# Backbone kernel on one core: where and when both mixers' first loads land, and the order of the first token tiles

## The chip, the cores and the metric

The program runs on one of the eight cores of a Trainium2 chip. A core has five engines with queues of their own: TensorE (PE, matmuls and transposes by an identity), VectorE (DVE), ScalarE (ACT), GpSimd (POOL) and SyncE (SP, which here issues loads only). DMA queues move data between HBM and the on-chip memory. An engine works its queue in order and waits at semaphores. The metric is the time of one execution on the device in microseconds, the median of several runs.

## The reference

Two layers over 512 latent tokens and 256 context tokens of width 1024, in float32. Each layer is a mixer, then a mixture of experts.

```python
for l in range(DEPTH):
    mod  = (silu(c) @ w_ada[l] + b_ada[l])          # six vectors of 1024; modc likewise from c_ctx
    h  = rms_norm(x, norm_w[l, 0]) * (1 + mod[1]) + mod[0]
    hc = rms_norm(ctx, norm_w[l, 0]) * (1 + modc[1]) + modc[0]
    yc, s_f, s_b = token_mixer(hc, w_in[l], ...)     # layer 1: only the states are wanted
    y, _, _      = token_mixer(h, w_in[l], ..., s_f, s_b)
    x = x + mod[2] * (y @ w_out[l])
    x = x + mod[5] * hier_moe(modulate(rms_norm(x, norm_w[l, 1]), mod[3], mod[4]))
    # layer 0 does the same two steps for ctx
return rms_norm(x, final_norm_w)

def token_mixer(h, w_in_l, ...):
    p = h @ w_in_l                                   # 1024 x 4096
    bg, cg, hv, q, zf_f, zf_b, iv, g = jnp.split(p, PROJ_SPLITS, axis=-1)
    # a gated short convolution of bg, cg, hv; a two-way recurrence of q, zf_f, zf_b, iv, gated by g
```

## The kernel before, in words

The 768 tokens are six tiles of 128 (four of x, two of ctx). A projection in float32 precision is made of three products of rounded parts: `split_w` (L312 to L323) loads a weight chunk of 512 KB into a `raw` tile, ACT casts it to a rounded high part (L319), and DVE or POOL subtracts that to get the low part (L322); both lie in a `hilo` tile. There are two `raw` buffers and four `hilo` buffers. The input is split likewise: `modulated` (L264) writes the high part of a token tile into H[0] = HA and H[1] = HB (four of the eight 128-wide blocks each) by ACT, and a low part by a POOL subtraction (L283), from a `mod` tile that DVE (and in layer 1 ACT for the first four blocks) makes. `proj_N` (L337) then does 24 matmuls for one token tile.

Each mixer starts with the same stage: normalise the tokens, transpose them on PE, modulate them, and project them on the value columns of w_in (`val`, L590, into Vn). I call it the value stage. After it come the head, gate and convolution projections, then the output projection, the router and the experts.

*Start of layer 0.* `setup` (L39) zeroes `rows` and fills it by seven small loads on SP's queue. `norm_first` (L285) loads each token tile on ACT's queue into one of two `xin` buffers, squares it on ACT (L256), makes its reciprocal root on DVE and POOL (L248, L249), multiplies on DVE (L261), transposes (L298) and copies to XT (L299), all six tiles ahead of the rest. `ada_step` (L199), eight times, loads a 1 MB slice of w_ada on SP's queue into one of three `adaw` buffers and multiplies it by the conditioning; after the eighth the result is transposed into the modulation columns (L222 to L242). Only behind these loads stand the first four chunks of w_in (`nat(6)`, L587).

*Start of layer 1.* The experts of layer 0 leave two rows for each token in `yb`, written by POOL's scatters. `combine` (L1577) loads them and adds both to X (L1588); `square`, `norm_next` (L302) and `modulated` follow. The order on DVE is written by hand (`manual_schedule`), so that tile i + 2 is added, and tile i + 1 multiplied and transposed, around the modulation of tile i. For the other engines the framework's scheduler sets the order, mostly that of the program. Two of the four weight chunks are split on DVE, two on POOL among the first tiles.

## Time and profile before

| | us |
|---|---|
| median of 3 runs (2002.50 to 2003.29) | 2002.74 |
| profiled execution, its own time | 1996.57 |
| its span in the trace | 1994.8 |
| mean granted TensorE clock | 0.945 |
| PE busy | 1700.2 (85% of the span) |
| DVE, ACT, POOL busy | 914.0, 458.2, 394.3 |

The span is that of one profiled execution; busy times are of its engines. A row of a timeline gives start, length, engine, source line and operation with output<-inputs; in brackets stands how long the engine was idle before it and what ended that. Several equal instructions are merged to one row (x12). The ends of matmuls are modelled, so a row of matmuls looks longer than the distance to the next row's start. The granted clock is a share of the full 2.4 GHz.

### The profile page before, as it was taken

How to read it: one execution, taken by the hardware profiler on the slowest of the kernel's cores; microseconds unless marked ns; L12 is line 12 of the kernel's file. 1: busy time of each engine (PE TensorE's matmuls, PEld its weight loads, DVE VectorE, ACT ScalarE, POOL GpSimd, SP SyncE). 2: the span in 40 equal slices, each digit the busy share in tenths (PEclk: the TensorE clock that was granted, in tenths of full speed). 3: DMA queues.
4: the chain of work that ended last, by engine and by line, in shares of the span. 5: the costliest groups of instructions: out<-in, count | busy, mean ns of one | idle time of the engine just before them, and what ended most of it. 6: DMA issues, size and time to landing. Idle time of an engine off the chain costs nothing. (4 is left out here: it accounts for less than half of the span.)

```text
span 1994.8 us, 33498 instructions
## 1 busy us (share of the span) xinstructions
PE 1700.2 (85%) x13488; PEld 1098.2 (55%) x13488; DVE 914.0 (46%) x2141; ACT 458.2 (23%) x897; POOL 394.3 (20%) x308
## 2 busy tenths in 40 slices
PE   5998999999968999888875899898968898888885
PEld 2766778798843444333332688777754344334342
DVE  4425255635664132222322637666563644445444
ACT  3512223323212122122211533333320100110011
POOL 1502212111122111111110632222111211111110
PEclk8999999999988999999987899999987999999998
DMA  7376562263489979999997322114478989999995
GB/s 276 101 271 212 179 212 76 76 242 90 168 326 374 418 317 379 417 416 418 417 419 298 135 82 57 54 43 157 137 280 324 417 342 417 418 417 418 417 418 241
DMA packets 141513, 542.35 MB, mean 272 GB/s; under 512 B 17394, under 2 KB 66720, under 8 KB 85417
## 3 DMA queue, kind: packets, MB, share of 16 engines
q1 hardware_dynamic: 118408, 466.17, 59.1%
q10 hardware_dynamic: 15040, 55.08, 8.0%
q0 software_dynamic: 7904, 18.90, 2.5%
q8 instruction: 108, 1.77, 0.4%
q14 instruction: 53, 0.43, 0.1%
HBM read 530.95 MB, written 15.96 MB: 274 GB/s over the span
## 5 line engine op out<-in xcount | busy, mean ns | idle before, releaser
L1230 PE MATMUL acc<-w,xT 128*32 128x256 f32 (+1 forms) x3360 | 378.4, 454 | 59.1 <-DVE xT L1213 34.6
L1230 PEld LDWEIGHTS acc<-w,xT 128*32 128x32 f32 (+1 forms) x3360 | 135.2, 119 | 260.6 <-issue 159.0
L322 POOL TENSOR_TENSOR hilo<-raw,hilo 128x1024 fp32r<-128x1024 f32 x64 | 157.3, 2463 | 436.4 <-ACT hilo L319 396.7
L333 PE MATMUL acc<-HA,hilo 128*128 128x384 f32 (+1 forms) x960 | 204.7, 355 | 0.0
L333 PE MATMUL acc<-HB,hilo 128*128 128x384 f32 (+1 forms) x960 | 202.4, 353 | 0.0
L333 PEld LDWEIGHTS acc<-HA,hilo 128*128 128x128 f32 x960 | 168.8, 189 | 16.2 <-issue 4.2
L333 PEld LDWEIGHTS acc<-HB,hilo 128*128 128x128 f32 x960 | 171.0, 190 | 9.2 <-issue 0.8
L1250 ACT COPY au<-acc 128x256 f32<-128x256 f32 (+1 forms) x69 | 31.1, 453 | 594.3 <-PE acc L1230 551.9
L345 PE MATMUL acc<-hilo,HA 128*128 128x512 f32 x504 | 131.2, 412 | 12.8 <-POOL HA L283 6.3
L1189 POOL DMA_INDIRECT xb<-h,idx x63 | 65.7, 1043 | 385.7 <-PE pS L1211 357.1
L345 PE MATMUL acc<-hilo,HB 128*128 128x512 f32 x504 | 125.8, 398 | 3.9 <-DVE hilo L322 3.6
L345 PEld LDWEIGHTS acc<-hilo,HA 128*128 128x128 f32 x504 | 97.9, 198 | 41.0 <-POOL HA L283 7.5
L1274 DVE SCALAR_TENSOR_TENSOR au<-w,gt,au 32x256 f32<-32x256 f32 (+2 forms) x102 | 58.6, 577 | 114.1 <-ACT au L1273 111.7
L319 ACT CAST hilo<-raw 128x1024 fp32r<-128x1024 f32 x80 | 83.5, 1049 | 119.1 <-PE acc L345 27.5
L345 PEld LDWEIGHTS acc<-hilo,HB 128*128 128x128 f32 x504 | 94.5, 190 | 29.1 <-DVE hilo L322 4.5
L1295 PE MATMUL acc<-w,hT 128*32 128x256 f32 (+1 forms) x816 | 97.2, 478 | 12.4 <-DVE hT L1258 6.4
L389 DVE TENSOR_TENSOR Q<-Q,Dk 128x256 f32<-128x256 f32 (+1 forms) x144 | 89.6, 651 | 23.7 <-PE pA L464 11.8
L1333 PE MATMUL acc<-w,hT 128*32 128x256 f32 (+1 forms) x896 | 87.4, 440 | 7.3 <-DVE hT L1258 5.2
L1181 POOL DMA_INDIRECT yb<-ys,idx x39 | 39.7, 1019 | 260.9 <-DVE ys L1297 185.3
L384 DVE TENSOR_TENSOR K<-K,Dk 128x768 f32<-128x768 f32 x64 | 72.9, 1139 | 21.5 <-ACT tmp L401 17.9
L1295 PEld LDWEIGHTS acc<-w,hT 128*32 128x32 f32 (+1 forms) x816 | 37.4, 126 | 69.5 <-issue 51.3
L1297 DVE TENSOR_TENSOR ys<-acc,au 128x256 f32<-128x256 f32 (+1 forms) x34 | 18.4, 542 | 124.9 <-PE acc L1295 124.5
(369 smaller groups left out, 2245.5 us busy)
## 6 DMA issues: line engine op xcount, KB each, us to landing
w<-in_w_e_gu SPq DMA_DIRECT2D x242, 1024.0 KB
w<-in_w_e_down SPq DMA_DIRECT2D x121, 1024.0 KB
adaw<-in_w_ada ACTq DMA_DIRECT2D x40, 1024.0 KB
raw<-in_w_in SPq DMA_DIRECT2D x64, 512.0 KB
adaw<-in_w_ada SPq DMA_DIRECT2D x8, 1024.0 KB
raw<-in_w_out SPq DMA_DIRECT2D x16, 512.0 KB
HA<-in_w_e_gu SPq DMA_DIRECT2D x6, 1024.0 KB
h<-SG SPq DMA_DIRECT2D x10, 512.0 KB
```

What stands on the lines that cost most here:

```text
L319: nc.scalar.copy(W[:, 0], w)
L322: eng.tensor_sub(W[:, 1], w, W[:, 0].bitcast(F32))
L333: nc.tensor.matmul(o, W[:, wi, k, :], H[k // 4][:, k % 4, hi, t], start=k == 0 and wi == hi, stop=k == 7 and wi == 1)
L345: nc.tensor.matmul(pa, H[k // 4][:, k % 4, hi, t], W[k // 2][:, wi, k % 2, :], start=k == ks[0] and wi == hi, stop=k == ks[-1] and hi == 1)
L384: nc.vector.tensor_tensor(half(Kv, TOK, 0, kn, b), half(Kv, TOK, 0, kn, b), vw(Dv, b, [[2 * b, n], [TOK - b, 2], [0, b]]), op=OP.mult)
L389: nc.vector.tensor_tensor(o, o, vw(Dv, (TOK + b) * d, [[2 * b, qn // (2 * b)], [0, b]]), op=OP.mult)
L1181: st = nc.gpsimd.indirect_dma_start(out=rows, out_offset=bass.IndirectOffsetOnAxis(ap=idx, axis=0), in_=yb, in_offset=None, bounds_check=r ...
L1189: self.nc.gpsimd.indirect_dma_start(out=xb, out_offset=None, in_=rows, in_offset=bass.IndirectOffsetOnAxis(ap=idx, axis=0), bounds_check=r ...
L1230: nc.tensor.matmul(pg[kind * u:kind * u + kind, :w], xT[k], gu[:, k % 2, w * u:w * u + w], start=st, stop=sp)
L1274: nc.vector.scalar_tensor_tensor(ms[pr, :o], self.m5s[pr, 0, c], g0[pr], ms[pr, :o], op0=OP.mult, op1=OP.add)
L1295: nc.tensor.matmul(py[kind * u:kind * u + kind, :w], hT[k], dn[k // 2][:, k % 2, w * u:w * u + w], start=k == 0, stop=k == 3)
L1333: nc.tensor.matmul(py[pr, :w], hT[k], dn[k // 2][:, k % 2, c], start=k == 0, stop=k == 3)
```

## The change

The first loads of both mixers get places of their own, and are issued in the order in which they are needed. Layer 0: the seven loads of `rows` become one load of an array that the host packs from seven small inputs by placing them in rows. The two first token tiles, the eight slices of w_ada, the four chunks of w_in and the other four token tiles stand in this order on SP's queue (`manual_schedule`), each with a buffer that nothing else holds: six slices lie where HA and HB will be, two chunks where SG will be, the token tiles in six tiles of their own. Tiles 0 and 1 are normalised first, tile i + 2 after tile i's modulation. Layer 1: the four chunks are loaded at once (two into SG's place) and all split on DVE; tile 0's add is made of two parts, tile 0's first low part goes to DVE, and the tiles follow each other with one tile's lead less. In both layers `val` asks for the products with the high part of the input first (`high`).

```diff
     def setup(self, consts, tmp, ps, dram, stp):
-        nc.gpsimd.memset(rows, 0.0)
-        q = nc.sync
-
-        def put(r, src):
-            q.dma_start(rows[r:r + src.shape[0], :], src)
-
-        put(0, io["c"].rearrange("a (r j) -> (a r) j", j=128))
...
+        nc.scalar.dma_start(rows, io["small"])
...
-    def modulated(self, l, i, H, src, pool):
+    def modulated(self, l, i, H, src, pool, eng=None):
...
-            nc.gpsimd.tensor_sub(H[h][:, :, 1, sl], mh, H[h][:, :, 0, sl].bitcast(F32))
+            (nc.gpsimd if h else eng or nc.gpsimd).tensor_sub(H[h][:, :, 1, sl], mh, H[h][:, :, 0, sl].bitcast(F32))
...
-    def proj_N(self, W, H, i, ps, group=range(4)):
+    def proj_N(self, W, H, i, ps, group=range(4), high=False):
...
-        for k in ks:
-            for hi, wi in ((0, 0), (0, 1), (1, 0)):
-                nc.tensor.matmul(pa, H[k // 4][:, k % 4, hi, t], W[k // 2][:, wi, k % 2, :], start=k == ks[0] and wi == hi,
-                                 stop=k == ks[-1] and hi == 1)
+        ms = [(k, hi, wi) for k in ks for hi, wi in ((0, 0), (0, 1), (1, 0))]
+        if high:
+            ms.sort(key=lambda m: (m[0] // 4, m[1]))
+        for m in ms:
+            k, hi, wi = m
+            nc.tensor.matmul(pa, H[k // 4][:, k % 4, hi, t], W[k // 2][:, wi, k % 2, :], start=m == ms[0], stop=m == ms[-1])
...
     def mixer(self, l, ps, st, ms):
-            HA = hy.tile([128, 4, 2, TOK], F32R, name="HA")
+            if l == 0:
+
+                aw = [t[:, i] for t in (hy.tile([128, 3, 2048], F32, name=n) for n in ("HA", "HB")) for i in range(3)]
...
+            def early():
+
+                w = [SG[:, 2 * u - 4:2 * u - 2, :] if u > 1 else
+                     wp.tile([128, 2, 512], F32, name="raw", bufs=self.raw_bufs) for u in range(4)]
+                for u in range(4):
+                    nc.sync.dma_start(w[u], win[256 * u:256 * u + 256, 512 * 6:512 * 7].rearrange("(k p) f -> p k f", p=128))
+                return w
...
                 if l == 0:
-                    XT = self.norm_first(H, p0, ps)
+                    aw += [p0.tile([128, 2048], F32, name="adaw", bufs=2) for _ in range(2)]
+                    XT = p0.tile([128, 8, TOK], F32, name="XT")
+                    xin = [p0.tile([128, D], F32, name=f"xin{i}") for i in range(6)]
+
+                    with tc.manual_schedule(engines={mybir.EngineType.SP}):
+                        for i in range(2):
+                            nc.sync.dma_start(xin[i], self.token_tile(i))
+                        for k in range(8):
+                            self.ada_load(0, 0, k, aw[k], nc.sync)
+                        ew = early()
+                        for i in range(2, 6):
+                            nc.sync.dma_start(xin[i], self.token_tile(i))
+                    for i in range(2):
+                        self.norm_first(i, xin[i], XT, p0, ps)
                     ast = {}
                     for k in range(8):
-                        self.ada_step(0, 0, k, ast, p0, ps, nc.sync, 3)
+                        self.ada_step(0, 0, k, ast, p0, ps, None, 2, aw[k])
                     self.ada_cols(0)
-                    W = nat(6)
+                    W = [self.split_w(None, wp, True, nc.vector if u % 2 else nc.gpsimd, ew[u]) for u in range(4)]
+                    inputs()
                     for i in range(6):
                         self.modulated(0, i, H, lambda k: XT[:, k, 128 * i:128 * i + 128], p0)
+                        if i + 2 < 6:
+                            self.norm_first(i + 2, xin[i + 2], XT, p0, ps)
                         val(W, i)
                 else:
-                    W = nat(6, range(2), nc.vector)
+                    inputs()
+                    ew = early()
 
                     with tc.manual_schedule(engines={mybir.EngineType.DVE}):
...
+                        W = [self.split_w(None, wp, True, nc.vector, w) for w in ew]
+                        for j in range(2):
+                            self.combine(0, 0, p0, (j,))
+                        sq = self.square(self.X[:, 0, :], p0)
+                        for i in range(6):
+                            pt = self.norm_next(sq, self.X[:, i, :], p0, ps)
+                            if i + 1 < 6:
+                                self.combine(0, i + 1, p0, (0,))
+                                if i:
+                                    self.combine(0, i + 1, p0, (1,))
+                            self.modulated(l, i, H, lambda k: pt[k // 4][:, 128 * (k % 4):128 * (k % 4) + 128], p0, nc.vector if i == 0 else nc.gpsimd)
+                            if i == 0:
+                                self.combine(0, i + 1, p0, (1,))
+                            if i + 1 < 6:
+                                sq = self.square(self.X[:, i + 1, :], p0)
+                            val(W, i)
```

**The order, first place: ACT at the start of layer 0.** Before, from the squares of the two context tiles on (hilo: weight casts; HA, HB: modulated high parts; modr: a store of the modulation rows):

```order
L256 ACTIVATE xn,ss<-xin 128x1024 x2
L319 CAST hilo<-raw 128x1024
L227 DMA modr_75<-adar 4x512 x2
L319 CAST hilo<-raw 128x1024
L274 ACTIVATE HA<-XT,mc_63,mA_67 128x128 x4
L274 ACTIVATE HB<-XT,mc_63,mA_67 128x128 x2
L319 CAST hilo<-raw 128x1024
L274 ACTIVATE HB<-XT,mc_63,mA_67 128x128 x2
L274 ACTIVATE HA<-XT,mc_63,mA_67 128x128
```

With the change, from the first weight cast on (SG: the third and fourth chunk's place; xin_167 is token tile 2):

```order
L310 CAST hilo<-raw 128x1024
L219 DMA modr_75<-adar 4x512 x2
L310 CAST hilo<-raw 128x1024
L310 CAST hilo<-SG 128x1024
L266 ACTIVATE HA<-XT,mc_63,mA_67 128x128
L310 CAST hilo<-SG 128x1024
L266 ACTIVATE HA<-XT,mc_63,mA_67 128x128 x3
L266 ACTIVATE HB<-XT,mc_63,mA_67 128x128 x4
L248 ACTIVATE xn,ss<-xin_167 128x1024
L266 ACTIVATE HA<-XT,mc_63,mA_67 128x128 x4
```

Three casts now stand ahead of tile 0's first activation, and the squares of later tiles stand between the tiles' activations.

**Second place: PE at the start of layer 1**, from the first transposes of normalised tokens (xn) on. Before:

```order
L309 MATMUL pS<-ident,xn 128x128 x8
L345 MATMUL acc<-hilo,HA 128x512 x12
L345 MATMUL acc<-hilo,HB 128x512
L309 MATMUL pS<-ident,xn 128x128 x8
L345 MATMUL acc<-hilo,HB 128x512 x11
L309 MATMUL pS<-ident,xn 128x128 x8
L345 MATMUL acc<-hilo,HA 128x512 x12
L345 MATMUL acc<-hilo,HB 128x512 x12
L309 MATMUL pS<-ident,xn 128x128 x8
```

With the change:

```order
L299 MATMUL pS<-ident,xn 128x128 x8
L340 MATMUL acc<-hilo,HA 128x512 x12
L340 MATMUL acc<-hilo,HB 128x512 x12
L299 MATMUL pS<-ident,xn 128x128 x8
L340 MATMUL acc<-hilo,HA 128x512 x12
L340 MATMUL acc<-hilo,HB 128x512 x12
```

The transposes of the next tile stood ahead of a tile's matmuls, and stand behind them now.

**Third place: DVE and POOL in the same stage.** X<-X,y are the two adds of a tile, rs<-ss and rs<-rs,nhalf the two halves of its reciprocal root, xn<-X,rs its product, mod<-pS four of its modulations, HA<-mod,HA and HB<-mod,HB the low parts. DVE before, from the adds of tile 2 on:

```order
L1588 TENSOR_TENSOR X<-X,y 128x1024 x2
L278 TENSOR_SCALAR mod<-pS,mA_68,mc_65 128x128 x4
L306 TENSOR_SCALAR xn<-X,rs 128x1024
L248 TENSOR_SCALAR rs<-ss 128x1
L1588 TENSOR_TENSOR X<-X,y 128x1024 x2
L278 TENSOR_SCALAR mod<-pS,mA_68,mc_65 128x128 x4
L306 TENSOR_SCALAR xn<-X,rs 128x1024
```

DVE with the change, from the product of tile 1 on:

```order
L296 TENSOR_SCALAR xn<-X,rs 128x1024
L1613 TENSOR_TENSOR X<-X,y 128x1024 x2
L270 TENSOR_SCALAR mod<-pS,mA_68,mc_65 128x128 x4
L240 TENSOR_SCALAR rs<-ss 128x1
L296 TENSOR_SCALAR xn<-X,rs 128x1024
L1613 TENSOR_TENSOR X<-X,y 128x1024 x2
```

POOL with the change, from the low part HB of tile 0 on:

```order
L275 TENSOR_TENSOR HB<-mod,HB 128x4x128
L241 TENSOR_TENSOR rs<-rs,nhalf 128x1 x2
L275 TENSOR_TENSOR HA<-mod,HA 128x4x128
L275 TENSOR_TENSOR HB<-mod,HB 128x4x128
L275 TENSOR_TENSOR HA<-mod,HA 128x4x128
L241 TENSOR_TENSOR rs<-rs,nhalf 128x1
L275 TENSOR_TENSOR HB<-mod,HB 128x4x128
```

Before, the adds of tile i + 2 preceded the modulation of tile i; now those of tile i + 1 follow the product of tile i, which waits for POOL's rs, and that stands behind HA's low part of the tile before.

## Rows read from the trace of the kernel before

**Rows 1.** Stage table: us, busy time of each engine, granted clock, DMA share, GB/s.

```profile
core 0: us, PE busy (x) PEld busy (x) DVE busy (x) ACT busy (x) POOL busy (x), PEclk, DMA share, GB/s
0.00:88.00 88.00, 61.24 (x264) 39.88 (x265) 46.84 (x120) 37.75 (x77) 29.77 (x37) 0.90 0.55 193
88.00:150.00 62.00, 61.21 (x340) 45.01 (x339) 11.10 (x15) 14.08 (x22) 9.34 (x5) 1.00 0.73 248
1080.00:1150.00 70.00, 48.59 (x265) 37.55 (x258) 39.11 (x57) 34.32 (x66) 36.48 (x23) 0.83 0.39 136
1150.00:1210.00 60.00, 56.53 (x453) 49.61 (x452) 30.50 (x42) 19.96 (x30) 18.77 (x8) 0.97 0.33 97
```

**Rows 2.** The same table, three short stretches.

```profile
10.00:20.00 10.00, 9.12 (x33) 3.60 (x33) 6.37 (x36) 3.56 (x7) 1.70 (x3) 1.00 0.94 368
...
56.00:62.00 6.00, 5.86 (x19) 4.74 (x20) 2.14 (x9) 0.99 (x3) 0.00 (x0) 0.72 0.66 175
...
1108.00:1113.00 5.00, 4.91 (x11) 3.52 (x12) 4.84 (x10) 1.86 (x4) 1.82 (x3) 0.50 0.73 244
```

**Rows 3.** Timeline, start of layer 0: start us, us, engine, line, operation [idle before <-releaser].

```profile
36.50 4.04 PE L217 MATMUL ada<-adaw,sT 128*32 128x512 f32 x24
...
43.77 11.18 DVE L278 TENSOR_SCALAR mod<-XT,mA,mc 128x128 f32<-128x128 f32 x16
...
54.87 1.21 DVE L322 TENSOR_TENSOR hilo<-raw,hilo 128x1024 fp32r<-128x1024 f32 x1
...
70.75 1.29 POOL L283 TENSOR_TENSOR HA<-mod,HA 128x512 fp32r<-128x512 f32 x1 [0.74 <-DVE mod L278]
...
71.29 2.88 PE L345 MATMUL acc<-hilo,HA 128*128 128x512 f32 x12
...
74.01 2.88 PE L345 MATMUL acc<-hilo,HB 128*128 128x512 f32 x12
...
87.61 2.27 PE L333 MATMUL acc<-HA,hilo 128*128 128x384 f32 x12
```

**Rows 4.** Tile views: duration ns min/median/max, first and last start.

```profile
L278 DVE TENSOR_SCALAR mod<-XT,mA,mc x48: 330/335/2448, 43.8 to 76.4; 128x128 f32<-128x128 f32 x48
...
L299 DVE COPY XT<-pS x12: 678/684/692, 12.8 to 36.6; 128x512 f32<-128x512 f32 x12
...
L1588 DVE TENSOR_TENSOR X<-X,y x12: 1212/1226/3261, 1094.8 to 1126.7; 128x1024 f32<-128x1024 f32 x12
...
L256 ACT ACTIVATE xn<-X x6: 1056/1060/1064, 1097.5 to 1128.0; 128x1024 f32<-128x1024 f32 x6
...
L306 DVE TENSOR_SCALAR xn<-X,rs x6: 742/746/1757, 1099.6 to 1133.8; 128x1024 f32<-128x1024 f32 x6
```

**Rows 5.** The page's costliest groups: busy us, mean ns of one | idle before, releaser.

```profile
L322 POOL TENSOR_TENSOR hilo<-raw,hilo 128x1024 fp32r<-128x1024 f32 x64 | 157.3, 2463 | 436.4 <-ACT hilo L319 396.7
...
L319 ACT CAST hilo<-raw 128x1024 fp32r<-128x1024 f32 x80 | 83.5, 1049 | 119.1 <-PE acc L345 27.5
```

**Rows 6.** Timeline, start of layer 1, columns as in the other.

```profile
1103.80 1.22 PE L345 MATMUL acc<-hilo,HA 128*128 128x512 f32 x2 [1.39 <-ACT HA L282]
...
1108.09 4.64 PE L345 MATMUL acc<-hilo,HA 128*128 128x512 f32 x10 [3.08 <-POOL HA L283]
...
1130.08 0.55 POOL L249 TENSOR_TENSOR rs<-rs,nhalf 128x1 f32<-128x1 f32 x1 [3.00 <-DVE rs L248]
...
1131.44 1.03 PE L309 MATMUL pS<-ident,xn 128*128 128x128 f32 x8
...
1131.64 0.59 ACT L591 COPY Vn<-acc 128x512 f32<-128x512 f32 x1 [1.43 <-PE acc L345]
...
1132.14 1.51 ACT L276 ACTIVATE mod<-pS,mc,mA 128x128 f32<-128x128 f32 x4
...
1133.67 0.62 ACT L282 CAST HA<-mod 128x512 fp32r<-128x512 f32 x1
...
1149.57 2.27 PE L333 MATMUL acc<-HA,hilo 128*128 128x384 f32 x12
```

More of the change, by code (lines that the diff above doesn't have):

```diff
@@ L213, in ada_step @@
                     nc.scalar.dma_start(nw[s:64:32, :], io["norm_w"][l, 1, :].rearrange("(j n) -> j n", n=512))
-        w = pool.tile([128, 2048], F32, name="adaw", bufs=bufs)
-        q.dma_start(w, io["w_ada"][l, 128 * k:128 * k + 128, 2048 * g:2048 * g + 2048])
+        if w is None:
+            w = self.ada_load(l, g, k, pool.tile([128, 2048], F32, name="adaw", bufs=bufs), q)
         for j in range(4):
@@ L590, in val @@
             def val(W, i):
-                nc.scalar.copy(Vn[:, i, :], self.proj_N(W, H, i, ps))
+                nc.scalar.copy(Vn[:, i, :], self.proj_N(W, H, i, ps, high=True))
+            def early():
[3 more added lines that the diff above has]
+                    nc.sync.dma_start(w[u], win[256 * u:256 * u + 256, 512 * 6:512 * 7].rearrange("(k p) f -> p k f", p=128))
+                return w
@@ L1575, in overflow, with combine @@
         self.scats = scats
-    def combine(self, l, i, cp):
+    def combine(self, l, i, cp, js=(0, 1)):
         nc = self.nc
-        y = cp.tile([128, 2, D], F32, name="y", bufs=3)
-        rows = self.ybs[l].rearrange("(t j) d -> t (j d)", j=2)[128 * i:128 * i + 128, :]
-        n = 1 if i else 2
-        for j in range(n):
-            nc.sync.dma_start(y.rearrange("p a b -> p (a b)")[:, 2 * D // n * j:2 * D // n * (j + 1)],
-                              rows[:, 2 * D // n * j:2 * D // n * (j + 1)])
+        if 0 in js:
+            y = cp.tile([128, 2, D], F32, name="y", bufs=3)
+            rows = self.ybs[l].rearrange("(t j) d -> t (j d)", j=2)[128 * i:128 * i + 128, :]
+            n = 1 if i else 2
+            for j in range(n):
+                nc.sync.dma_start(y.rearrange("p a b -> p (a b)")[:, 2 * D // n * j:2 * D // n * (j + 1)],
+                                  rows[:, 2 * D // n * j:2 * D // n * (j + 1)])
+            self.ycur = y
         x = self.X[:, i, :]
-        for j in range(2):
-            nc.vector.tensor_add(x, x, y[:, j, :])
+        for j in js:
+            nc.vector.tensor_add(x, x, self.ycur[:, j, :])
     def finish(self):
@@ L1760 @@
         io[name] = nc.dram_tensor(f"in_{name}", a.shape, _mybir.dt.from_np(a.dtype), kind="ExternalInput").ap()
+    small = _np.zeros((128, 128), _np.float32)
+    for r, n in ((0, "c"), (8, "c_ctx"), (16, "norm_w"), (48, "conv_w"), (72, "conv_norm_w"), (80, "hg_lb"), (96, "hg_norm_w")):
+        a = _np.asarray(inputs[n]).reshape(-1, 128)
+        small[r:r + a.shape[0]] = a
+    arrays["in_small"] = small
+    io["small"] = nc.dram_tensor("in_small", small.shape, F32, kind="ExternalInput").ap()
     out = nc.dram_tensor("out", (1, SEQ, D), F32, kind="ExternalOutput").ap()
```

66 lines of the change are left out of this document (22 added, 44 removed).

## The prediction

> **What bounds the kernel now.** I read the stage table first [rows 1]: it shows where TensorE (PE) is not the bound. From 88 to 150 us it is busy 61.21 of 62 us, from 1150 to 1210 us 56.53 of 60. In the two stretches that the change touches it is not: 61.24 of 88 us at the start of layer 0, 48.59 of 70 at the start of layer 1. So what the two starts win or lose moves the full stretches behind them, and the end, one for one. Then the timelines of the two starts [rows 3, 6], for when the value stage (six token tiles through `val`, 24 matmuls each) ends and what it waits for. In layer 0 the last w_ada matmul ends at 36.50 + 4.04 = 40.54 us, the first modulated tile starts at 43.77, the value stage hands over to the next projection at 87.61 us. 144 matmuls at 2.72 us per 12 (the two starts in [rows 3]) are 32.6 us, so some 11 us of the 43.8 are waits. In layer 1 tile 0's matmuls start at 1103.80, stop after two, and go on at 1108.09; the stage ends at 1149.57. Last the tile views [rows 4], for durations and above all for their spread: a VectorE (DVE) modulation from SBUF takes 0.33 us and once 2.45, an X add 1.21 and once 3.26, an xn product 0.74 and once 1.76. The reader is to see that DVE and GpSimd (POOL) hold each other up for a whole instruction: 2.45 is a POOL split [rows 5]. In the steady tiles of layer 0 POOL works 1.29 us, then waits 0.74 for four modulations [rows 3]: 0.185 each, and one after the other. I therefore add their times wherever both have SBUF work.
>
> **Layer 0, step by step.** The seven small `rows` loads become one; the first transposes wait for tokens in any case, so this counts as nothing: its cover is the 1 MB of tokens ahead of it, and without that it costs what 1 MB takes at the rate below, 2.7 us at most. That w_ada lies in HA's and HB's place costs nothing either: nobody writes there before PE has read it.
>
> *Loads.* Up to the last w_ada slice 9.5 MB (two token tiles of 0.52, eight slices of 1.05, the packed rows) now stand in front with no buffer to wait for. Between 10 and 20 us the queues moved 368 GB/s at 0.94 busy [rows 2], 390 if full: 24.4 us, and some 2 us until the first bytes flow, so 26.4 us (25 to 28.5). The last slice's four matmuls take 0.67 (a sixth of 4.04), and 43.77 − 40.54 = 3.23 lead to modulated tile 0: 30.3 instead of 43.77. The Trainium skill's page "DMA: Bandwidth & Descriptors" (Where 436 GB/s comes from) puts a core's HBM share at about 358 GB/s; by that the last slice lands 2.1 us later. Measured here is more, so the sum stays at 390.
>
> *First weights.* Their 0.52 MB chunks follow; from 56 to 62 us such loads ran at 175/0.66 = 265 GB/s [rows 2]: 1.3 to 2 us each, so they land at 28.0, 29.6, 31.2, 32.8. The ACT order puts three casts (1.05 [rows 5]) ahead of tile 0's first activation: 31.2 + 1.05 gives 32.3. That is 2 us lost of the 13.5. Tokens 2 to 5 come behind the weights on SP's queue, from 34 us on; ACT squares tile 2 after tile 0's eight activations, past 36 us, so this is hidden; without that cover each tile would wait 1.4 to 2 us.
>
> *DVE against POOL.* From there POOL has the third chunk's split (2.46) and two residuals (1.29 each), DVE 16 modulations (3.0) and two splits (1.21 each): 10.5 us, in turn; four modulations may already be done (−0.7). Then rs and power (0.7), POOL's next residual (1.29), and xn of tile 2 (0.75), for which PE waits inside tile 0: 44.8. Eight transposes (1.05) and the last six matmuls (1.4) end tile 0 at 47.3.
>
> *The rest.* Five tiles at 5.44 and three more sets of transposes, 30.4 us. The loop now makes xn(i+2) between tiles; for tile 4 the way from one set of transposes to the next is 1.05 + two XT copies (0.68 each) + six modulations 1.1 + rs and power 0.7 + two residuals 2.6 + 0.75 = 7.6 us, while PE has 1.05 + 16 matmuls, 4.7: 2.9 us of wait, 3 with the next tile's. End 47.3 + 30.4 + 3 = 80.7 instead of 87.6: **−6.9 us**. Bounds: −14, if the turns of DVE and POOL fall into gaps and PE paces from 33 us; −3, if loads run at the low rate and each turn is in series. I take the serial sum, since before it held: the 16 modulations begun at 43.77 took 11.18 us and let the second DVE split in at 54.87 [rows 3], the time of their own 3.0 and of POOL's two splits and three residuals beside them, 4.9 + 3.9.
>
> **Layer 1, step by step.** The y loads still wait for the last scatter, so tile 0's add stays at 1094.8 [rows 4] and its first matmul at 1103.80. The weights' four splits go to DVE into the idle time before y; the two that POOL did among the X adds vanish, and tile 0's first residual is on DVE. The loads of y for tiles 4 and 5 now stand behind loads for the next projection; they are needed past 1125 only, so nothing is counted. So tile 0 runs through: 11 matmuls at 0.46 (the slow pitch from 1108.09), 13 at 0.227: ends at 1111.7.
>
> *What is new* stands in PE's order: transposes of tile i now come after the matmuls of tile i−1, where they stood ahead of them. From the transposes PE waits for the Vn copy and four modulations on ACT (+0.70 to their start, 1.51 long) and the cast (0.62) before tile i can begin: a tile takes 0.70 + 1.51 + 0.62 + 5.44 = 8.3 us, where matmuls and transposes alone, 5.44 + 1.03, set the pace [rows 3, 6].
>
> *And a longer ring* stands in the orders of DVE, POOL and ACT. The add of X(i+1) follows xn(i) on DVE; xn(i) needs its power, which POOL does after the residual of HA(i−1); and ACT has the square of X(i+1) ahead of Vn(i−1) and the modulations of tile i. One turn: Vn 0.50, modulations 1.53, cast 0.62, residual HA 1.29, power 0.55, residual HB 1.29, xn 0.75, two adds 2.45, square 1.06 [rows 3, 4, 6]: 10.0, with eight hand-overs **10.3 us a tile**. PE's 8.3 hides under it. Tile 1: transposes from 1111.7, matmuls 3.9 later (its modulations, a square, its cast), end 1121.1; modulations of tile 2 at 1123.3, of tile 3 at 1133.6, of tile 4 at 1143.9. Tile 5 has no add: 1143.9 + 2.2 + 5.44 + 0.70 = 1152.2, and 7.6 more: 1159.9 instead of 1149.6, **+10.3 us**. Bounds: +4.7, if only PE's bubble is paid; +18, if PE also runs slow (below).
>
> **Behind the starts.** The new order of matmuls (`high`) frees the first weight buffer after 10 matmuls of the last tile instead of 6, 0.9 us later. Its next cast and POOL split (1.05 + 2.46) then end some 5.8 us into that tile, just when PE, done at 5.44 and two matmuls on, asks for them: 0, at most 0.9 a layer. The queues of the rest stand as before.
>
> **Sum**: −6.9 + 10.3 = +3.4 us. The profiled execution, 1996.57 us (span 1994.8), becomes 2000.0; the median of the runs shown stands 6.17 above it, so **2006.1 us**.
>
> **Rivals.**
> *A, both starts pay.* DVE and POOL fall into each other's gaps: layer 0 then is paced by PE, −14, and layer 1 pays only the bubble, +4.7: 1993.4. For it: most modulations took 0.33, the spread shows only some waits. Against: POOL's regular 0.74 us waits [rows 3]. It decides if a tile of layer 1 takes under 9 us.
> *B, half of it.* One ring is shorter than counted: −8.5 and +7: 2001, no change.
> *C, slower by the clock.* From 1108 to 1113 us the granted clock was 0.50 [rows 2], the lower level (1.2 GHz), after PE had done two matmuls and waited 3 us; ten matmuls took 4.64 us. The new order leaves PE 2.9 to 3.8 us idle in each of five tiles of layer 1. If half of each tile's matmuls then run at 0.46, that is 12 × 0.23 = 2.8 us a tile, of which the ring hides 10.3 − 8.3 = 2.0, while slow transposes add 0.5: four tiles at 1.3 and the last in full, +8: 2014. It decides once an idle stretch is as long as that one. The Trainium skill's page "TensorE: Matmul & The Clock Gate" (HAM oscillation) says that a loop whose waits let the clock fall pays the slow restart every turn; by that rule C would come about, and the trace bears it out for one gap only.
> *D, the change doesn't do what it says.* If SG's two loads in layer 1 wait for the last scatter as y does, they go ahead of y: 1.05 MB at 390 are 2.7 us, 2009.
>
> **How the numbers follow.** 0.2% (4.0 us) is about what a measurement can tell from no change. My forecast has 0.42; its own range is 2002 to 2011, 0.24 of it inside 4 us and 0.18 above. A 0.27, B 0.13, C 0.12, D 0.06. Faster: A, 0.27. Same: 0.24 + 0.13 = 0.37. Slower: 0.18 + 0.12 + 0.06 = 0.36. The range reaches into A and to C: 1992 to 2014.
>
> **What would show it.** Right: the value stage of layer 0 ends near 81 us with the last w_ada slice landing near 26; in layer 1 POOL's residuals repeat every 10 us, PE's waits in the value stage name ACT's HA cast, the stage ends some 10 us later counted from the last scatter. Wrong: tiles of layer 1 under 9 us apart, layer 0 under 76 us (A), a granted clock of 0.5 in the middle of layer 1's tiles (C), SG's loads issued beside y's (D).

## The result, and the profile after

The changed kernel takes 2014.50 us (median of 10 runs, 2012.36 to 2022.69) where the kernel before takes 2003.59 in the same comparison (10 runs, 1999.89 to 2007.54): ratio 1.0072, 95% interval 1.0056 to 1.0089, so it is **slower by 11 to 18 us**; by the medians it is 10.9. Forecast were +3.4 us and 2006.1; the range ended at 2014.0. (The ratio compares runs made in turn and is not quite the quotient of the two medians; in what follows both are given.)

The profiled execution took 2015.04 us, span 2013.2, against 1996.57 and 1994.8: 18.4 us more. That is more than the times show, because the traced execution of the kernel before is a fast one, 7.0 us under the median of its ten runs, while that of the changed kernel is at its median. The stage table of the changed kernel, with the stretches of [rows 1] (us, busy time of each engine, granted clock, DMA share, GB/s):

```profile
0.00:88.00 88.00, 62.10 (x305) 44.98 (x306) 43.58 (x120) 40.56 (x81) 34.93 (x37) 0.94 0.55 205
88.00:150.00 62.00, 59.89 (x323) 41.70 (x325) 11.53 (x15) 11.05 (x18) 5.50 (x4) 0.97 0.74 253
1080.00:1150.00 70.00, 42.78 (x227) 31.51 (x224) 37.40 (x52) 24.54 (x47) 15.55 (x14) 0.76 0.43 154
1150.00:1210.00 60.00, 55.68 (x260) 47.92 (x259) 19.33 (x28) 21.58 (x37) 17.50 (x10) 0.94 0.21 62
```

At the start of layer 1 PE is busy 42.78 of 70 us where it was 48.59, at a granted clock of 0.76 instead of 0.83. That is a loss, but a table of fixed stretches does not tell how large: everything behind a loss moves through them. For that I cut each trace at events that both kernels have, and compare the laps between them. L0: to the first matmul behind layer 0's value stage. A: to the first transposes of gathered tokens, `xb`, where the experts begin. B: to the first transposes of `xw`, a few experts later. C: to layer 0's last down projection. L1: to the first matmul behind layer 1's value stage. R: to the end. Each lap is the difference of two start times in PE's timeline (the kernels e1 to e9 are described below; each row is one execution):

```
               L0     A      B      C      L1    R       span
before         87.6   489.3  84.6   423.7  64.4  845.2   1994.8
changed        80.0   494.1  95.4   422.4  79.6  841.7   2013.2
e1_place       83.3   493.4  84.7   421.7  80.0  846.8   2009.9
e2_before_pl.  87.9   493.5  92.1   422.6  64.4  843.0   2003.6
e3_l1old       81.4   489.7  93.2   422.5  64.5  848.1   1999.3
e4_l1old_place 84.7   491.6  84.7   421.4  65.7  851.1   1999.2
e5_lead        81.2   494.0  95.1   422.5  79.7  846.6   2019.1
e6_warm        81.5   492.2  92.8   422.6  72.4  847.0   2008.4
e7_lead_warm   80.2   498.2  94.3   422.9  71.5  851.3   2018.4
e8_l0          81.2   488.4  84.7   424.6  66.1  842.3   1987.3
e9_hybrid      80.2   492.0  85.2   422.6  61.6  848.5   1990.1
```

The 18.4 us are −7.6 (L0), +4.8 (A), **+10.8 (B)**, −1.3 (C), **+15.2 (L1)** and −3.5 (R). The prediction had terms for L0 and L1 and none for A, B, C and R.

**L0 went as forecast.** PE's timeline of the changed kernel at the start of layer 0 (start, length, engine, line, operation, idle before it):

```profile
25.99 1.06 PE L209 MATMUL ada<-adaw,sT 128*32 128x512 f32 x8 [1.44 <-DMA adaw<-in_w_ada]
...
31.68 0.82 PE L340 MATMUL acc<-hilo,HA 128*128 128x512 f32 x2 [3.10 <-ACT HA L266]
...
45.31 1.63 PE L340 MATMUL acc<-hilo,HB 128*128 128x512 f32 x6
...
56.30 1.06 PE L289 MATMUL pS<-ident,xn 128*128 128x128 f32 x8 [2.17 <-DVE xn L253]
...
80.02 2.64 PE L324 MATMUL acc<-HA,hilo 128*128 128x384 f32 x12
```

The last w_ada slice lets its matmuls go at 25.99 (forecast: landing at 26.4), tile 0 ends at 45.31 + 1.5 = 46.8 (47.3), tile 4's transposes wait 2.17 us for xn (2.9), and the stage ends at 80.02 (80.7; before 87.61 [rows 3]). One premise did not hold, at no cost here: of the slices that were to have no buffer to wait for, the last two (`adaw`) are issued only at 13.62 us, after a wait of 7.3 us.

**L1 lost more than forecast.** The same view at the start of layer 1, to be read beside [rows 6]:

```profile
1108.49 1.94 PE L299 MATMUL pS<-ident,xn 128*128 128x128 f32 x8 [14.64 <-DVE xn L296]
1111.82 5.49 PE L340 MATMUL acc<-hilo,HA 128*128 128x512 f32 x12 [1.39 <-ACT HA L274]
1117.11 3.12 PE L340 MATMUL acc<-hilo,HB 128*128 128x512 f32 x12
1120.07 1.03 PE L299 MATMUL pS<-ident,xn 128*128 128x128 f32 x8
1123.86 4.61 PE L340 MATMUL acc<-hilo,HA 128*128 128x512 f32 x12 [2.75 <-ACT HA L274]
...
1133.96 4.61 PE L340 MATMUL acc<-hilo,HA 128*128 128x512 f32 x12 [1.87 <-ACT HA L274]
...
1144.06 4.60 PE L340 MATMUL acc<-hilo,HA 128*128 128x512 f32 x12 [1.87 <-ACT HA L274]
1148.50 2.92 PE L340 MATMUL acc<-hilo,HB 128*128 128x512 f32 x12
1151.27 1.03 PE L299 MATMUL pS<-ident,xn 128*128 128x128 f32 x8
1154.17 4.61 PE L340 MATMUL acc<-hilo,HA 128*128 128x512 f32 x12 [1.87 <-ACT HA L274]
...
1171.48 2.27 PE L324 MATMUL acc<-HA,hilo 128*128 128x384 f32 x12
```

A tile takes 1144.06 − 1133.96 = 10.1 us, which is what was forecast (10.3). But the 12 HA matmuls of each tile take 4.4 us, the 12 HB matmuls 2.8: in every tile from tile 1 on the clock falls some 0.7 us behind the wait for the cast (the granted clock is 0.50, the level of 1.2 GHz, from 1135 to 1138 us), and comes back. So some 7 of a tile's 24 matmuls run at the low clock. The windows of one tile's two halves (the first number behind the POOL column is the granted clock):

```profile
1134.00:1138.00 4.00, 4.00 (x11) 3.16 (x12) 2.19 (x2) 0.43 (x1) 3.01 (x3) 0.58 0.00 2
1138.00:1141.00 3.00, 3.00 (x15) 2.46 (x14) 1.92 (x2) 0.95 (x1) 0.00 (x0) 0.99 0.00 0
```

And the timeline of ACT in two tiles of the same stretch shows that the forecast ring is there as well:

```profile
1141.36 0.59 ACT L590 COPY Vn<-acc 128x512 f32<-128x512 f32 x1 [0.15 <-PE acc L340]
...
1150.15 1.06 ACT L248 ACTIVATE xn<-X 128x1024 f32<-128x1024 f32 x1 [5.62 <-DVE X L1613]
...
1151.46 0.59 ACT L590 COPY Vn<-acc 128x512 f32<-128x512 f32 x1 [0.16 <-PE acc L340]
```

The square that the ring makes late ends 0.16 us before PE has the next Vn ready. Ring and slow PE reach the same instruction at the same time, so this trace alone cannot say which of them sets the pace.

**B was not in the forecast at all.** The timeline of SP's queue in layer 0's experts, of the kernel before (w: expert weights, 1 MB a load; start, length from the first of the merged loads to the last):

```profile
583.79 3.69 SPq L1162 DMA_DIRECT2D w<-in_w_e_gu  x4
588.01 0.87 SPq L1162 DMA_DIRECT2D w<-in_w_e_down  x2
589.70 25.76 SPq L1162 DMA_DIRECT2D w<-in_w_e_gu  x4
615.65 1.02 SPq L1162 DMA_DIRECT2D w<-in_w_e_down  x2
```

The same of the changed kernel:

```profile
581.07 4.99 SPq L1185 DMA_DIRECT2D w<-in_w_e_gu  x4
613.96 0.87 SPq L1185 DMA_DIRECT2D w<-in_w_e_down  x2
```

Both queues stand still until some 614 us. But before, four more loads had gone out by then: the two w_e_down at 588.01 and two of the four in the merged row at 589.70, which spans the wait. The view of waits of the changed kernel's SP queue names the reader, a down projection on PE (us in total, times, longest), and PE's timeline shows that its last matmuls read HB and end at 613.89:

```profile
SPq L1185 <- PE acc L1318: 27.7, 1, 27.7
```

```profile
611.54 2.35 PE L1318 MATMUL acc<-HB,hT 128*32 128x256 f32 x32
```

Meanwhile the DMA queues run dry. One window of 10 us in the table of windows, first of the kernel before, 410 GB/s, then of the changed one, 86:

```profile
600.00:610.00 10.00, 6.45 (x86) 4.97 (x89) 6.53 (x27) 3.50 (x9) 1.56 (x2) 0.50 1.02 410
```

```profile
600.00:610.00 10.00, 6.45 (x79) 4.36 (x81) 7.22 (x28) 4.63 (x11) 0.70 (x1) 0.50 0.26 86
```

PE pays some 30 us later, in the changed kernel's timeline:

```profile
643.19 3.60 PE L1253 MATMUL acc<-w,xT 128*64 128x512 f32 x8 [5.91 <-DMA w<-in_w_e_gu]
...
658.43 1.94 PE L1253 MATMUL acc<-w,xT 128*32 128x256 f32 x16 [2.76 <-DMA w<-in_w_e_gu]
```

Where does this come from, 500 us behind the last edited line of layer 0? The pool `hy` hands out memory in the order in which tiles are first asked for. Before that order was HA, YC, HB. The change asks for HA and HB first, because w_ada's slices lie there, and for YC after. HA and HB take 24 KB of a partition, YC 12 KB, so HB's place now begins 12 KB lower. Later the same place HB holds weights of the static experts, which PE's down projection reads last, and an expert tile `w1` of another pool takes 8 KB of which, by the compiled program's list of places (no view of these runs shows it), the upper half was the lowest third of YC's place. By that list, before it waited only for the tiles in HA's and YC's places; with the change it reaches into HB's, and waits for HB's last reader. It is the fifth load of the group, a w_e_down, and the loads behind it in SP's queue go out after it. That the order of the three places makes this wait is what e1 and e2 test.

### The profile page after: what moved, and what is told of

It is laid out like the page before. It is cut to its first block, busy times and chain, and to the rows that moved or that the text cites. A ratio compares the mean times of both kernels' runs of the same rounds, so it can differ in the third digit from the quotient of the medians.

```text
span 2013.2 us, 33459 instructions
## 1 busy us (share of the span) xinstructions
PE 1705.7 (85%) x13488; PEld 1100.8 (55%) x13488; DVE 910.6 (45%) x2144; ACT 457.6 (23%) x897; POOL 382.8 (19%) x304
## 5 line engine op out<-in xcount | busy, mean ns | idle before, releaser
L1253 PE MATMUL acc<-w,xT 128*32 128x256 f32 (+1 forms) x3360 | 383.5, 460 | 65.1 <-DVE xT L1236 32.2
L313 POOL TENSOR_TENSOR hilo<-raw,hilo 128x1024 fp32r<-128x1024 f32 x61 | 149.3, 2453 | 445.8 <-ACT hilo L310 404.8
L340 PE MATMUL acc<-hilo,HA 128*128 128x512 f32 x504 | 139.0, 430 | 21.4 <-ACT HA L274 11.6
L340 PEld LDWEIGHTS acc<-hilo,HA 128*128 128x128 f32 x504 | 101.8, 207 | 52.7 <-ACT HA L274 13.2
L340 PE MATMUL acc<-hilo,HB 128*128 128x512 f32 x504 | 124.3, 396 | 0.6 <-DVE hilo L313 0.6
L310 ACT CAST hilo<-raw 128x1024 fp32r<-128x1024 f32 x76 | 79.3, 1050 | 128.9 <-PE acc L340 43.9
L340 PEld LDWEIGHTS acc<-hilo,HB 128*128 128x128 f32 x504 | 94.8, 190 | 24.8 <-issue 4.2
L383 DVE TENSOR_TENSOR Q<-Q,Dk 128x256 f32<-128x256 f32 (+1 forms) x144 | 91.8, 666 | 25.0 <-PE pA L458 11.8
L1320 DVE TENSOR_TENSOR ys<-acc,au 128x256 f32<-128x256 f32 (+1 forms) x34 | 18.4, 543 | 133.5 <-PE acc L1318 133.1
```

Of the source, the lines that this page charges most:

```text
L310: nc.scalar.copy(W[:, 0], w)
L313: eng.tensor_sub(W[:, 1], w, W[:, 0].bitcast(F32))
L340: nc.tensor.matmul(pa, H[k // 4][:, k % 4, hi, t], W[k // 2][:, wi, k % 2, :], start=m == ms[0], stop=m == ms[-1])
L383: nc.vector.tensor_tensor(o, o, vw(Dv, (TOK + b) * d, [[2 * b, qn // (2 * b)], [0, b]]), op=OP.mult)
L1253: nc.tensor.matmul(pg[kind * u:kind * u + kind, :w], xT[k], gu[:, k % 2, w * u:w * u + w], start=st, stop=sp)
```

## The experiments

All comparisons are ratios to the kernel before, run in turn on the same chip; in brackets stands the 95% interval. The first four put one part back at a time.

**e1_place**, the change with YC's place between HA's and HB's again in layer 0:

```diff
-                aw = [t[:, i] for t in (hy.tile([128, 3, 2048], F32, name=n) for n in ("HA", "HB")) for i in range(3)]
+                a0 = hy.tile([128, 3, 2048], F32, name="HA")
             YC = hy.tile([128, 4, TOK], F32, name="YC")
+            if l == 0:
+                a1 = hy.tile([128, 3, 2048], F32, name="HB")
+                aw = [t[:, i] for t in (a0, a1) for i in range(3)]
```

> The change with one thing put back: in layer 0 the place of YC is taken between HA and HB again, as before the change. Theory P (places): with the change HB's place begins 12 KB lower and overlaps the place of a later expert weight tile (w1), so the load of that tile, and the 4 loads behind it on SP's queue, wait for the last reader of the weights that lie in HB; the stretch from 614 to 673 us lost 7.4 us by it. Then the waits for weights on PE at 643 and 658 us (5.91 and 2.76 us) go, and the time falls by 7 us to about 2007.5. Rival N: those waits are the scatter of one execution's transfers; then the long wait of SP's queue stays (27.7 us) or the time stays at 2014.5 within 2 us.

Measured: 1.0048 (1.0028 to 1.0068), 2010.95 us, so 3.5 us less than the changed kernel by the medians and 4.8 by the ratios; theory P had 2007.5. Lap B is 84.7 again, and the fifth and following loads go out as before, in the timeline of e1's SP queue:

```profile
588.89 0.87 SPq L1188 DMA_DIRECT2D w<-in_w_e_down  x2
590.57 26.45 SPq L1188 DMA_DIRECT2D w<-in_w_e_gu  x4
```

Neither theory foresaw why it is not 7: lap L0 is 3.3 longer. The waits of e1's SP queue in the first 40 us show the reason:

```profile
SPq L188 <- DVE lbo L78: 11.3, 1, 11.3
```

And its timeline there:

```profile
1.64 1.39 SPq L188 DMA_DIRECT2D HA<-in_w_ada  x3
14.43 1.29 SPq L188 DMA_DIRECT2D HB<-in_w_ada  x3
```

Slices of w_ada that go to HB's old place wait for one of the setup's small tiles, `lbo`, until 14.4 us, and from 10 to 20 us the queues move 274 GB/s where the changed kernel moves 420. The same 12 KB help layer 0's start and hurt its experts.

**e2_before_place**, the mirror: the kernel before, with HA, HB, YC in layer 0.

```diff
             HA = hy.tile([128, 4, 2, TOK], F32R, name="HA")
+            if l == 0:
+                HB = hy.tile([128, 4, 2, TOK], F32R, name="HB")
             YC = hy.tile([128, 4, TOK], F32, name="YC")
-            HB = hy.tile([128, 4, 2, TOK], F32R, name="HB")
+            if l:
+                HB = hy.tile([128, 4, 2, TOK], F32R, name="HB")
```

> The kernel before with only the order of three places altered in layer 0: HA, HB, YC as with the change, in place of HA, YC, HB. Theory P: the same expert load waits for the same reader, SP's queue shows one wait of 23 to 28 us and PE a wait of some 6 us for weights near 640 us, and the time rises by 7 us to 2010.5. Rival N: no such wait, 2003.6 within 2 us.

Measured: 1.0040 (1.0024 to 1.0057), 2009.80 against 2003.40: +6.4 us. Apart from waits at semaphores, no engine's instructions or their order in the stretches told of here differ from the kernel before; the wait of SP's queue is there, and PE's behind it, in the views of waits and the timeline of e2:

```profile
SPq L1165 <- PE acc L1298: 26.9, 1, 26.9
```

```profile
647.61 3.52 PE L1233 MATMUL acc<-w,xT 128*64 128x512 f32 x8 [5.71 <-DMA w<-in_w_e_gu]
```

Lap B is 92.1, L0 and L1 are those of the kernel before. Theory P holds, in both directions.

**e3_l1old**, the change with layer 1's start as before (loads, splits, order of tiles, order of the products), and **e4_l1old_place**, that with e1's edit too.

```diff
-                    ew = early()
+                    W = nat(6, range(2), nc.vector)
...
-                        W = [self.split_w(None, wp, True, nc.vector, w) for w in ew]
-                        for j in range(2):
-                            self.combine(0, 0, p0, (j,))
...
+                        for i in range(-2, 6):
...
-                nc.scalar.copy(Vn[:, i, :], self.proj_N(W, H, i, ps, high=True))
+                nc.scalar.copy(Vn[:, i, :], self.proj_N(W, H, i, ps, high=l == 0))
```

> The change with the start of layer 1 (loads, splits, order of tiles, order of the products) as before; layer 0's start and places as changed. Theory L (layer 1's order costs 15 us, from the last expert's down projection to the end of the value stage): the time falls by 15 to 2000, and from that down projection to the end of the value stage it is again 64.4 us. Rival M: a good part of layer 1's loss is only moved there from layer 0's experts, then it falls by under 11 us.

> Both put back: YC's place between HA and HB, layer 1's start as before; what is left is layer 0's start. Theories P and L together: 2014.5 - 7 - 15 = 1992.5, which is 11 below before, more than layer 0's start gave at 80 us (7.6), so some of it must be lost on the way: 1993 to 1999. Rival: layer 0's gain does not reach the end, since the experts of layer 0 wait for their weights in any case: 2003.6 within 2 us.

Measured: e3 1.0013 (0.9995 to 1.0030), 2004.40 us; e4 0.9990 (0.9972 to 1.0009), 2001.12. Lap L1 is 64.5 and 65.7, where it is 79.6 and 80.0 with the change's order: 14 to 15 us, as theory L had it. L's time, 2000, is missed by 4.4: the medians fall by 10.1 and 9.8 only, under the 11 that rival M named (the ratios by 0.59 and 0.58%, which is 11.8 and 11.6 us). But M's reason is not there, since lap C in front of L1 is the same within 1 us (421.4 to 422.5). Lap R is longer with the old order, 848.1 and 851.1 against 841.7 and 846.8. That lap holds what the last section calls scatter. e4's forecast, 1993 to 1999, is missed by 2 us, for the reason found in e1: its L0 wins 2.9 us, not 7.6.

The next three ask what sets the 10.1 us a tile in layer 1: the ring, or PE with a fallen clock.

**e5_lead** takes adds and square out of the ring:

```diff
                         for i in range(6):
+                            if i and i + 1 < 6:
+                                for j in range(2):
+                                    self.combine(0, i + 1, p0, (j,))
                             pt = self.norm_next(sq, self.X[:, i, :], p0, ps)
-                            if i + 1 < 6:
+                            if i == 0:
                                 self.combine(0, i + 1, p0, (0,))
-                                if i:
-                                    self.combine(0, i + 1, p0, (1,))
```

> The change with one alteration in layer 1's start: from tile 2 on both adds of a tile stand on DVE ahead of the xn product of the tile before, so that add and square leave the ring Vn, modulation, cast, low part, power, xn, two adds, square, Vn. With the change a tile takes 10.1 us, and two things come to the same: that ring (10.0; ACT idles 0.16 us ahead of Vn) and PE's own turn (transposes 1.03, wait for the cast 1.87, 24 matmuls of which half at the low clock 7.2). Theory R (the ring alone sets the pace): a tile takes 8.3 to 9, from first matmul to the end of the stage 59.7 falls to 51 to 54. Theory C (PE with its fallen clock sets it as well): a tile stays at 10.1, 59.7 within 1.

Measured: 1.0088 (1.0062 to 1.0114). From first matmul to the stage's end 59.8 us (59.7 with the change), and a tile still takes 10.1, in PE's timeline of e5:

```profile
1145.12 4.60 PE L340 MATMUL acc<-hilo,HA 128*128 128x512 f32 x12 [1.87 <-ACT HA L274]
...
1155.23 4.60 PE L340 MATMUL acc<-hilo,HA 128*128 128x512 f32 x12 [1.87 <-ACT HA L274]
```

The edit did open the ring. The square now ends early, and ACT, which idled 0.16 us ahead of Vn with the change, idles 3.19 us there, in ACT's timeline of e5:

```profile
1142.42 0.59 ACT L590 COPY Vn<-acc 128x512 f32<-128x512 f32 x1 [3.19 <-PE acc L340]
```

With the ring open nothing moves, so the ring alone does not set the pace. Theory C.

**e6_warm** fills PE's wait instead:

```diff
             nc.tensor.transpose(pt[k // 4][:, 128 * (k % 4):128 * (k % 4) + 128], xn[:, 128 * k:128 * k + 128], self.ident)
+        d = ps.tile([128, 512], F32, name="ada", bufs=1)
+        for k in range(13):
+            nc.tensor.transpose(d[:, :128], xn[:, 128 * (k % 8):128 * (k % 8) + 128], self.ident)
         return pt
```

> The change with 13 transposes more after each tile's eight in layer 1's start (of the same xn into a PSUM tile that nobody reads; some 1.7 us at the full clock), which fill PE's wait of 1.87 us for the cast. Tile 0's are in the cold and delay it by up to 2 us. Theory C alone: the granted clock stays at 1.0 in the tiles, PE's turn is 8.4, and the stage ends 5 to 8 us sooner (59.7 becomes 52 to 55). Theory R alone: a tile stays at 10.0, PE waits for xn instead, and 59.7 stays within 2. Both bounds together: as R.

Measured: 1.0051 (1.0032 to 1.0069). The stage takes 52.8 us instead of 59.7, with 78 transposes more work. Tiles 1 to 3 in PE's timeline of e6 (L343 is the changed kernel's L340):

```profile
1118.00 3.03 PE L343 MATMUL acc<-hilo,HA 128*128 128x512 f32 x12 [1.33 <-ACT HA L274]
...
1127.44 3.03 PE L343 MATMUL acc<-hilo,HA 128*128 128x512 f32 x12 [1.40 <-ACT HA L274]
...
1137.30 4.28 PE L343 MATMUL acc<-hilo,HA 128*128 128x512 f32 x12 [1.81 <-ACT HA L274]
```

The HA half takes 2.9 us while the clock holds. But PE still waits 1.33 to 1.81 us behind the added transposes, tiles are 9.4 and 9.9 us apart, and behind the third wait the clock falls once more. ACT's timeline of e6 shows what PE waits for:

```profile
1133.57 1.06 ACT L248 ACTIVATE xn<-X 128x1024 f32<-128x1024 f32 x1 [5.66 <-DVE X L1616]
...
1134.62 0.56 ACT L593 COPY Vn<-acc 128x512 f32<-128x512 f32 x1
```

The square waits for DVE's adds, Vn follows it without idle time, and the squares are 9.9 and 9.8 us apart (1123.71, 1133.57, 1143.40). So the ring is a second bound, at about 9.4 to 9.9, close under the first; only the last tile, behind which there is nothing to add, comes at 8.48 (1147.38 to 1155.86).

What was expected of two bounds (as theory R, 59.7 within 2) was missed. 2.7 of the 6.9 us are tile 0: the added transposes take its slow start upon themselves, so its matmuls, all at the full clock, take 5.57 us (1108.64 to 1114.21) instead of 8.25, and start 0.4 us later for it. The other 4.2 lie behind tile 0.

**e7_lead_warm** has both edits.

> Both alterations of the two kernels before: adds one tile ahead, and 13 transposes more per tile. If ring and clock each give 10 us a tile, only this one falls: a tile takes 8.3 to 9, 59.7 becomes 51 to 54, and the time falls by 6 to 8 from 2014.5. If either one alone sets the pace, this equals that one's kernel.

Measured: the stage takes 50.0 us, and from tile 2 on the tiles are 8.5 to 8.7 apart at a granted clock of 1.00, in PE's timeline of e7:

```profile
1144.39 3.12 PE L343 MATMUL acc<-hilo,HA 128*128 128x512 f32 x12 [0.45 <-ACT HA L274]
...
1153.01 3.02 PE L343 MATMUL acc<-hilo,HA 128*128 128x512 f32 x12 [0.45 <-ACT HA L274]
```

The two bounds are thus shown one by one: opening the ring alone wins 0, holding the clock alone 6.9, both 9.7 of the 13.9 us that the stage lost (59.7 against 45.8). Tile 0 has 2.7 and 2.4 of that (in e7 its matmuls start 1.0 us later). Behind tile 0 the stage takes 51.4 us with the change, 51.5 in e5, 47.2 in e6 and 44.1 in e7. The other 4.2 are not taken apart by any run: a tile of e7 takes 8.5 us where a steady tile before took 6.35 (1125.88 to 1132.23), which is the bubble in PE's order, while before pays for a stall in tile 0 [rows 6] that e7 does not have. In the time of the whole kernel e7 shows none of this: 1.0065 (1.0041 to 1.0088, 5 runs from 2009 to 2020 us) is no better than the change. That part of the forecast failed. Its trace, which is of the slowest of the five, has laps A and R, in which it runs the change's own instructions, 4.1 and 9.6 us longer than the changed kernel's; whether the other four lost as much there is not known.

The last two look for a version that keeps the gain.

**e8_l0**: layer 0's start of the change, layer 1's start of before, the places HA, YC, HB of before in both layers, and w_ada's slices in the order HA's place, the two `adaw` tiles, HB's place, so that the three that must wait for the setup are last.

```diff
-                    aw += [p0.tile([128, 2048], F32, name="adaw", bufs=2) for _ in range(2)]
+                    aw = [a0[:, i] for i in range(3)] + [p0.tile([128, 2048], F32, name="adaw", bufs=2) for _ in range(2)] + [a1[:, i] for i in range(3)]
```

> Layer 0's start alone, with its places mended: HA, YC, HB lie as before the change in both layers, and w_ada's slices go to HA's place (3), the two adaw tiles, then HB's place (3), so that those that must wait for the setup's tiles at the end of memory (till 14.4 us) are the last in the queue; layer 1's start as before the change. Layer 0's value stage ends at 80 to 81.5 us, the experts' start takes 84.7 us to the last static expert as before, layer 1's start 64.4 to 65.7. 2003.5 - 7 = 1996.5, 1994.5 to 1999. Rival: what the start gains is lost behind it, 2001 to 2004.

Measured: 0.9972 (0.9955 to 0.9989), 1994.61 against 2000.72 us: **6 us faster than before**, and inside the forecast. The three slices still wait until 14.39 us, but with five slices ahead of them the queues do not run dry, and the last lands as early as with the change (its matmuls start at 25.89). SP's queue in e8:

```profile
4.76 0.80 SPq L188 DMA_DIRECT2D adaw<-in_w_ada  x2
14.39 1.28 SPq L188 DMA_DIRECT2D HB<-in_w_ada  x3
```

L0 is 81.2, B 84.7. What the start of layer 0 wins does reach the end.

**e9_hybrid** adds to e8 two pieces of the change in layer 1, the early loads with all four splits on DVE and the products with the high part first, and keeps the old order of tiles.

```diff
-                    W = nat(6, range(2), nc.vector)
+                    ew = early()
...
+                        W = [self.split_w(None, wp, True, nc.vector, w) for w in ew]
...
-                            if i == -2:
-                                W += nat(6, range(2, 4), nc.gpsimd)
```

> Layer 0's start with mended places, as in the kernel before this, and in layer 1 two pieces of the change without its order of the tiles: the four weight chunks loaded at once and split on DVE ahead of y, and the products with the high part first; transposes stay ahead of the matmuls of the tile before, adds two tiles ahead. POOL no longer splits weights among the first X adds, so PE's wait of 3.07 us after two matmuls goes: from first matmul to the end of the stage 45.8 becomes 40.5 to 43, the time falls by 3 to 5 from 1994.6, to 1990 to 1992. Rival: the two loads in SG's place delay the last scatter and y by what is won (16.6 to 17 us to the first transposes instead of 15.2), or tile 0 stays in the cold as long: 1994 to 1996.

Measured: 0.9950 (0.9929 to 0.9970), 1994.10 against 2001.53 us: **0.5% under the kernel before**, the lowest ratio of all. The stall of [rows 6] (two matmuls, then 3.08 us) is gone, in PE's timeline of e9:

```profile
1101.35 5.37 PE L340 MATMUL acc<-hilo,HA 128*128 128x512 f32 x12 [2.28 <-ACT HA L274]
1106.55 0.39 PE L340 MATMUL acc<-hilo,HB 128*128 128x512 f32 x1
```

From first matmul to the stage's end it takes 40.2 us instead of 45.8, a little more gain than forecast. Tile 0 is still slow: its 12 HA matmuls take 5.2 us, and start 0.9 us later behind the transposes than in e8. The forecast of the time, 1990 to 1992, was missed; 1994.10 lies in the rival's 1994 to 1996. e8 and e9 were not run in the same comparison, nor on the same chip, and their intervals overlap: e9 beats e8 in lap L1 (61.6 against 66.1), and the times do not tell them apart.

## Why the prediction was wrong, step by step

- *Layer 0's start, −6.9*: right, −7.6. The serial sum of DVE's and POOL's work was the right choice between its bounds. The loads were sized well: in the first 10 us the queues moved 315 GB/s, where 2 us of nothing and 390 after it come to 312, and from 10 to 20 us 420, not 390. The 358 GB/s of the Trainium skill's page "DMA: Bandwidth & Descriptors" (Where 436 GB/s comes from), which the prediction set aside, is no bound here: 420 are measured.
- *Behind the starts, "the queues of the rest stand as before"*: **the step that failed first.** SP's instructions do stand as before, in the same order; what a load waits for does not. The sentence "that w_ada lies in HA's and HB's place costs nothing either: nobody writes there before PE has read it" looked at who uses the place during the start, and not at where the place lies. It costs 10.8 us in lap B of this trace (7.5 in e2, 8.6 in e3), 6.4 in the times of e2, and was priced at 0.
- *Layer 1's start, +10.3*: the direction and the pace were right, the reason was half right and **the term was too small**: +15.2 in lap L1. The ring of ten microseconds exists (e6 shows it at 9.4 to 9.9), and e7 shows that opening it wins 2.8 us more than the clock alone; but e5 shows that it was not the only bound. The prediction took PE's turn as 8.3 us, which "hides under" the ring. With some 7 of a tile's 24 matmuls at the low clock (4.4 us for the first half, 2.8 for the second) PE's turn is 1.03 + 1.87 + 7.2 = 10.1. The clock then costs where no ring hides it: tile 1's and the last tile's turns, 1.8 us each, worked out from 7.2 against 5.44. The rest of the 4.9 are the first transposes, 1.3 us later behind the last down projection (16.6 instead of 15.2), where the prediction has "tile 0's add stays at 1094.8". SG's two loads are the likely cause. In the four traces in which they are issued 2.2 us ahead of the last scatter (the changed kernel, e5, e6, e7), tile 0's square starts 10.1 to 11.5 us behind that scatter; where they are issued 3.9 us ahead of it (e1, e9), 9.6 and 9.8; with the old loads (before, e2, e3, e4, e8), 9.6 to 9.7. No run tests that alone. (e4 and e8 also have some 17 us from the down projection to the transposes, but there the down projection itself takes 3.2 and 3.6 us instead of 1.9.)
- *Rival C*, the clock, had 0.12: it came about in every tile from tile 1 on, behind waits of 1.87 us, shorter than the 3.08 from which it was to decide. That its time, 2014, lies beside the measured 2014.50 is luck: it had nothing for the places. The prediction took the one gap that the trace of before shows as the measure of how long a gap must be. The rule of the Trainium skill that it cited (page "TensorE: Matmul & The Clock Gate", HAM oscillation: a loop whose waits let the clock fall pays the restart each turn) was right about the mechanism: five tiles paid it, 1.6 us each. *Rival D* as it was put is out: SG's loads do not wait for the last scatter; they are issued at 1092.45, it at 1094.62. What they may cost all the same, 1.3 us, stands above; D had 2.7.
- *The sum.* −7.6 + 10.8 + 15.2 are 18.4, and laps A, C and R add 4.8 − 1.3 − 3.5 = 0. In times, which scatter more: the change is at +0.72%, of which the order of layer 1 is 0.58 to 0.59 (the changed kernel against e3, e1 against e4), the places 0.23 to 0.24 net of the 3.3 us that they help L0 (against e1, e3 against e4), and layer 0's start with YC's old place −0.10 (e4); these three make up the whole. With the slices in another order as well that start is at −0.28 (e8).

What stays open: laps A and R vary by up to 10 us between kernels that run the same instructions there, and R is 841.7 to 847.0 in four of the five kernels with the change's order in layer 1, but 848.1 and 851.1 in e3 and e4. The granted clock goes with it in part (from 1175 to 1420 us the mean is 1.00 in the changed kernel, 0.97 in e7 and e4, but 1.00 in e6 too, whose R is 847.0), and why one execution loses the clock behind a wait and another does not was not tried.

## What to carry to other kernels

A tile that is asked for earlier in a pool moves every place behind it, and with it what loads far down the program wait for; an order of instructions that is unchanged does not show this, so compare also what each load of a full queue waits for. A loop that makes PE wait a little in each turn has two prices, the wait and the clock behind it, and the second can make the first bound look like another engine's ring: open both before deciding which it was. And where a rearrangement wins in one place and loses in another, take it apart: here layer 0's part, with the slices in another order, wins 0.3%, that with two pieces of layer 1's part 0.5% (the two are not told apart by time), and the whole loses 0.7%.

## What the runs showed of the hardware that was not expected

- The clock can fall behind short waits. Behind waits of 1.87 us on PE, 12 matmuls took 4.4 us instead of 2.8 in each tile of the changed kernel from tile 1 on (granted clock 0.58 over 4 us); behind 0.45 us (e7) it stayed at 1.00, behind 1.33 and 1.40 us (e6) the matmuls kept their 2.85 us, behind 1.81 (e6) they did not. It is not the length of the wait alone: elsewhere in layer 1, in PE's timeline of the kernel before, a wait of 2.06 us is followed by matmuls at a granted clock of 1.00 (window 1354 to 1358 us):

```profile
1354.99 0.46 PE L410 MATMUL pS<-Q,tmp 128*32 128x32 f32 x32 [2.06 <-DVE Q L389]
1355.38 0.96 PE L333 MATMUL acc<-HA,hilo 128*128 128x512 f32 x3
```

- 13 transposes whose result nobody reads, in each of six tiles, make the stage 6.9 us shorter (e6), 6.4 counted from its first transposes: work that fills a wait can be worth more than the time it takes.
- Time of the whole kernel is a poor measure of such a stage. e7 wins 8.1 us in lap L1 and shows nothing in the total. Executions differ by as much in stretches that nobody touched (lap A is 489.7 to 498.2 in the changed kernel, e3, e5, e6 and e7, which run the same instructions there), though it is not shown that this alone hides the gain. Laps between equal events agree far better (B: 84.6 to 85.2 in the five kernels with the old places; from layer 1's first matmul to the stage's end 45.8 in all five with the old start there).
